# Conv taps, mean and activation at other places in the hand-written order of a two-layer hybrid trunk

## The chip, the cores and the metric

The kernel runs on one core of one Trainium2 chip. The metric is device time in microseconds (us) of one execution, compared by medians of several runs. The core has five engines with a queue of instructions each, which an engine works through in order: PE (matrix products; its weight loads are listed apart as PEld), DVE (vector operations), ACT (scalar functions, copies, squares), POOL and SP. SP's queue issues nearly all loads. [...]

## What is computed

Two layers. Each has a mixer with three branches that read the same normalised input h, each branch under a gate of its own, and then a gated feed-forward part with a width-3 convolution:

```
h = modulate(rms_norm(x, mix_norm_g[l]), sh1, sc1)
z = h @ w_in        # -> MLA latents, MoBA qkv, conv input, 3*D gate logits
o_a = causal_attention(...) @ w_mla_o                    # MLA branch
o_b = moba_attention(...) @ w_moba_o                     # MoBA branch
u = glu_a * sigmoid(glu_g)                               # conv branch
u = causal_depthwise_conv(u, conv_dw_w, conv_dw_b)       # width 31, 512 channels
u = silu(layer_norm(u, conv_ln_g, conv_ln_b))
o_c = u @ w_conv_pw2 + b_conv_pw2
merged = g[0] * o_a + g[1] * o_b + g[2] * o_c            # g = sigmoid(gate logits)
x = x + g1 * (merged @ w_out)
x = x + g2 * channel_mixer(modulate(rms_norm(x, ffn_norm_g[l]), sh2, sc2))
```

D is 1024, the sequence 256, the batch 1, all float32. `sh1, sc1, g1, sh2, sc2, g2` come from `silu(c) @ w_mod[l] + b_mod[l]`, one row of 6 × 1024 for each layer.

## The kernel before

Activations lie transposed on the chip, channels on the 128 partitions and the 256 positions along the row. Every float32 product is made of three: a weight tile and an activation are each split in a high part and a remainder, and PE forms high × high (L300), remainder of the activation × high weight (L301) and high × remainder of the weight (L303). Weights come in units of 512 KB (128 × 1024): SP loads one into one of four buffers `raw` (L199), ACT writes its high part `whi` (L222), DVE the remainder `wlo` (L224), three units ahead of the one in use. A unit of the gates is 24 matmuls on PE.

What stands where is written by hand: `STEPS` is one list of tokens for each layer, and the program is emitted in that order; the framework then orders each engine's queue by it and by what waits for what. Tokens that matter here:

- G51 is the first half of gate pair 5 (one unit), C31 a unit of the conv branch's gate, O5 a unit of the MLA and MoBA output products (`out_ab`), OC0 a pw2 product of the conv branch (`out_c`, four k-steps that read `uh` and `ul`), PR0 a step of the product with w_out. BA and MA are the two attentions, RW prepares the row `crow`.
- v0 and v1 mark a stretch of the list. `_spread` puts the conv's taps into it, 4 taps a token, evenly by the units of PE work. A tap is one DVE instruction (L1103); the 124 taps of a layer are 4 channel blocks × 31.
- r0 and r1 mark the stretch of the row products R: DVE multiplies a row of w_mod with `crow` and sums it (L390), then adds the bias (L391). There are 16 in layer 0 and 8 in layer 1 within the mixer. Each needs a load of 512 KB.
- m0 and m1 mark the stretch of M, four small matmuls of a k-step of the modulation (L407) on a tile `in_wm` that is loaded into a `raw` buffer.
- LN is `conv_mean`: three adds on DVE (L1113 to L1115), the mean by a matmul (L1116), four subtractions on DVE (L1121). LS is `conv_rstd`: four squares on ACT, three adds on DVE (L540, L535, L540), a sum over channels on PE (L545), L519 on DVE, a power on POOL (L520). LB is `conv_silu`: the broadcast on PE (L555), then for each of four blocks L1135 and L1140 on DVE around ACT's tanh, `uh` on ACT (L1141) and `ul` on DVE (L1142).

So the conv branch runs as a chain between DVE, PE and ACT while PE goes on with units of gates and outputs; where its instruction on PE comes up before DVE has delivered, PE stands.

Of the kernel before, what the change touches and what calls it, by code (L numbers as in the profile page):

```python
# [76 lines left out]
    "GLU0 GLU1 GLU2 GLU3 LE0 LE1 LR0 QKV00 LR1 LT QKV01 QKV02 QKV03 UQ UK QKV10 MS0 QKV11 MS1 QKV20 QKV12 "  # L77
    "QKV13 QKV21 MP0 MP1 m0 QKV22 v0 MA00 MA01 MA10 MA02 BS0 MA03 MA04 C00 MA11 BS1 BP0 BP1 QKV23 C01 MA12 "
    "MA13 C10 BA00 BA01 C11 MA14 BA02 G00 C20 BA03 BA10 BA11 BA12 C21 C30 BA13 G01 G10 G11 O0 G20 RW0 G21 G30 "
    "O1 O2 G31 G40 G41 O3 v1 RW1 RW2 RW3 O4 G50 C31 LN G51 G60 O5 LS G61 r0 LB O6 G70 G71 OC0 PR0 OC1 OC2 O7 "  # L80
    "OC3 OC4 PR1 PR2 OC5 m1 PR3 PR4 OC6 OC7 PR5 PR6 PR7 r1 "
), (
    "GLU0 GLU1 GLU2 GLU3 KL0 KL1 KL2 KL3 KL4 KL5 KL6 KL7 LE0 LE1 LR0 QKV00 LR1 LT QKV01 UQ QKV02 UK QKV03 MS0 "
    "QKV10 QKV11 v0 QKV12 MS1 QKV13 QKV20 MP0 QKV21 QKV22 MP1 QKV23 BS0 m0 MA00 MA10 C00 MA01 BS1 MA02 C01 MA11 "
    "MA03 C10 MA04 MA12 m1 C11 MA13 BP0 C20 BP1 MA14 C21 BA00 BA01 G00 BA02 BA10 G01 BA03 BA11 G10 v1 "
    "BA12 C30 G11 C31 BA13 O0 O1 G20 RW0 LN G21 G30 RW1 RW2 RW3 G31 O2 G40 r0 G41 G50 O3 LS G51 LB G60 O4 O5 G61 "
    "OC0 G70 OC1 PR0 OC2 OC3 PR1 OC4 OC5 G71 O6 O7 PR2 OC6 PR3 OC7 PR4 r1 PR5 PR6 PR7 "
)]

# [1335 lines left out]
```

## Time and profile before

| | us |
|---|---|
| median of 3 runs | 907.75 |
| lowest and highest | 905.73, 909.30 |
| the profiled execution, whole | 909.82 |
| its span between first and last instruction | 907.7 |

The profile's granted clock of PE has a mean of 0.996. The costliest groups of instructions are the weight split on ACT and DVE and the three product lines on PE:

```profile
L222 ACT ACTIVATE whi<-raw 128x1024 fp32r<-128x1024 f32 (+2 forms) x286 | 296.6, 1043 | 217.6 <-PE psb L301 117.3
L224 DVE TENSOR_TENSOR wlo<-raw,whi 128x1024 fp32r<-128x1024 f32 (+2 forms) x286 | 340.3, 1195 | 65.5 <-ACT whi L222 57.9
L300 PE MATMUL psb<-hh,whi 128*128 128x256 f32 x1088 | 263.5, 282 | 0.5 <-ACT p L675 0.3
L1103 DVE SCALAR_TENSOR_TENSOR cacc<-upad,cw,cacc 128x256 f32<-128x256 f32 x240 | 105.7, 477 | 0.4
```

A row reads: line, engine, operation, result and operands, shape, how often; busy us and mean ns of one; idle time of the engine just before such an instruction, and what ended most of it. A matmul's busy time overlaps the next one's, so the distance from one start to the next says more of PE. In a timeline, a row gives start and duration in us, and in brackets the idle time ahead of it with what ended it.

### The profile page before, as it was taken

Reading aid. Unit: us, or ns where it says so; the run is one execution under the profiler, and the core shown is the slowest. Engines: PE = TensorE matmul, PEld = TensorE weight load, DVE = VectorE, ACT = ScalarE, POOL = GpSimd, SP = SyncE. Lnnn points to the kernel's source line nnn. Section 1 sums busy time; section 2 is a strip of 40 time slices with the busy share of each in tenths; the row PEclk is TensorE's granted clock in tenths of the full one; section 3 lists DMA queues with packets and bytes.
Section 4 is the critical chain, followed back from the end, with each engine's and each line's share of the span. In section 5 each row is a group of like instructions: output and inputs, shape, how many; then the busy total and the mean of one; then the engine's idle time right before and its main releaser. Section 6 shows DMA issues by size and latency. Waiting matters only on the chain.

```text
span 907.7 us, 18736 instructions
## 1 busy us (share of the span) xinstructions
PE 888.3 (98%) x7339; PEld 841.5 (93%) x7339; DVE 797.1 (88%) x1554; ACT 555.2 (61%) x979; POOL 46.2 (5%) x36
## 2 busy tenths in 40 slices
PE   7999999999999999999999999999999999999998
PEld 6888888999998999999989988989999899999998
DVE  6989999999988999998764999999887798777774
ACT  4677588644755655556543676986475565565551
POOL 1010700000000000000000043000000000000000
PEclk9999999999999999999999999999999999999999
DMA  8956535699988889996633664157768676566631
GB/s 321 379 196 202 187 118 183 214 334 320 304 292 308 295 296 312 313 301 211 200 112 108 197 223 161 53 184 244 264 206 270 221 259 189 186 194 199 190 92 47
DMA packets 57976, 201.59 MB, mean 222 GB/s; under 512 B 6944, under 2 KB 8480, under 8 KB 57888
## 3 DMA queue, kind: packets, MB, share of 16 engines
q1 hardware_dynamic: 57888, 200.41, 66.6%
q8 instruction: 57, 0.93, 0.4%
q14 instruction: 31, 0.25, 0.1%
HBM read 199.33 MB, written 1.05 MB: 221 GB/s over the span
## 4 chain that ended last, share of the span: by engine, by line
PE 78%; DVE 12%; ACT 4%; DMA 3%; issue 2%; SPq 0%; POOL 0%; POOLq 0%; DVEq 0%; ACTq 0%
PE psb L300 16%; PE psb L301 16%; PE psb L303 15%; PE psa L300 7%; PE psa L301 7%; PE psa L303 7%; DVE wlo L224 3%; DVE cacc L1103 3%; PE psa L407 2%; DVE raw L778 1%; ACT whi L222 1%; PE psa L294 1%; DVE raw L390 1%; DMA raw<-in_win 1%; ACT p L675 1%
## 5 line engine op out<-in xcount | busy, mean ns | idle before, releaser
L222 ACT ACTIVATE whi<-raw 128x1024 fp32r<-128x1024 f32 (+2 forms) x286 | 296.6, 1043 | 217.6 <-PE psb L301 117.3
L224 DVE TENSOR_TENSOR wlo<-raw,whi 128x1024 fp32r<-128x1024 f32 (+2 forms) x286 | 340.3, 1195 | 65.5 <-ACT whi L222 57.9
L300 PE MATMUL psb<-hh,whi 128*128 128x256 f32 x1088 | 263.5, 282 | 0.5 <-ACT p L675 0.3
L301 PE MATMUL psb<-hl,whi 128*128 128x256 f32 x1088 | 261.0, 280 | 0.0
L300 PEld LDWEIGHTS psb<-hh,whi 128*128 128x128 f32 x1088 | 205.0, 189 | 6.3 <-issue 3.8
L301 PEld LDWEIGHTS psb<-hl,whi 128*128 128x128 f32 x1088 | 205.0, 189 | 0.5 <-DVE wlo L224 0.4
L303 PE MATMUL psb<-hh,wlo 128*128 128x256 f32 x1088 | 149.2, 279 | 0.0
L303 PEld LDWEIGHTS psb<-hh,wlo 128*128 128x128 f32 x1088 | 135.6, 188 | 0.8 <-issue 0.8
L1103 DVE SCALAR_TENSOR_TENSOR cacc<-upad,cw,cacc 128x256 f32<-128x256 f32 x240 | 105.7, 477 | 0.4
L300 PE MATMUL psa<-mhl,whi 128*128 128x256 f32 x400 | 94.0, 278 | 0.0
L301 PE MATMUL psa<-mhl,whi 128*128 128x256 f32 x400 | 93.7, 278 | 0.0
L1300 DVE SCALAR_TENSOR_TENSOR e<-psb,fw,e 128x255 f32<-128x255 f32 (+1 forms) x176 | 84.0, 477 | 5.4 <-ACT e L1298 4.5
L520 POOL TENSOR_TENSOR rs<-rs,mhalf 128x8 f32<-128x8 f32 (+3 forms) x26 | 44.6, 1729 | 669.2 <-DVE rs L519 669.1
L300 PEld LDWEIGHTS psa<-mhl,whi 128*128 128x128 f32 x400 | 75.0, 188 | 0.0
L301 PEld LDWEIGHTS psa<-mhl,whi 128*128 128x128 f32 x400 | 75.0, 188 | 0.0
L1298 ACT ACTIVATE e<-psb,fb,fw 128x256 f32<-128x256 f32 x88 | 48.5, 551 | 22.4 <-DVE e L1300 19.2
L390 DVE SCALAR_TENSOR_TENSOR raw<-raw,crow 128x1024 f32<-128x1024 f32 x48 | 58.5, 1218 | 0.5 <-DMA raw<-in_wmr 0.5
L303 PE MATMUL psa<-mhl,wlo 128*128 128x256 f32 x400 | 53.9, 277 | 0.0
L303 PEld LDWEIGHTS psa<-mhl,wlo 128*128 128x128 f32 x400 | 49.4, 188 | 0.0
L1308 ACT ACTIVATE mhl<-e 128x256 fp32r<-128x256 f32 x44 | 18.3, 416 | 30.1 <-DVE e L1306 27.6
L300 PE MATMUL psb<-whi,hh 128*128 128x416 f32 (+1 forms) x96 | 30.9, 350 | 4.5 <-ACT hh L854 4.5
L301 PE MATMUL psb<-whi,hl 128*128 128x416 f32 (+1 forms) x96 | 29.6, 343 | 0.2 <-DVE hl L855 0.2
(275 smaller groups left out, 1474.3 us busy)
## 6 DMA issues: line engine op xcount, KB each, us to landing
raw<-in_wup SPq DMA_DIRECT2D x88, 512.0 KB, 4.9
raw<-in_wmr SPq DMA_DIRECT2D x60, 512.0 KB, 5.7
raw<-in_wdn SPq DMA_DIRECT2D x44, 512.0 KB, 4.5
raw<-in_wm SPq DMA_DIRECT2D x32, 512.0 KB, 4.7
raw<-in_wgab SPq DMA_DIRECT2D x32, 512.0 KB, 4.9
raw<-in_wqkv SPq DMA_DIRECT2D x24, 512.0 KB, 5.1
raw<-in_win SPq DMA_DIRECT2D x16, 512.0 KB, 4.7
raw<-in_wgc SPq DMA_DIRECT2D x16, 512.0 KB, 4.3
```

The source lines that it names most:

```text
L222: ac.activation(hi, raw, AF.Copy)
L224: ve.tensor_tensor(lo, raw, hi.bitcast(F32), op=ALU.subtract)
L300: te.matmul(o, p1[0], p1[1], start=start, stop=False)
L301: te.matmul(o, p2[0], p2[1], start=False, stop=False)
L303: te.matmul(o, p3[0], p3[1], start=False, stop=stop)
L390: ve.scalar_tensor_tensor(raw, raw, scale, row, op0=ALU.mult, op1=ALU.mult, accum_out=acc)
L407: te.matmul(acc[32 * c:32 * c + 32, 0:S], cact[:, k:k + 1].to_broadcast([P, 32]), raw[:, c * S:(c + 1) * S], start=(k == 0), stop=(k == KD ...
L520: gp.tensor_tensor(r, r, mhalf[:, :n], op=ALU.pow)
L1103: ve.scalar_tensor_tensor(aj, upad[:, j, t:t + S], cw[:, j * 31 + t:j * 31 + t + 1], aj, op0=ALU.mult, op1=ALU.add)
L1298: ac.activation(t, src, AF.Identity, scale=fw[:, 2, c:c + 1], bias=fb[:, c:c + 1])
L1300: ve.scalar_tensor_tensor(t[:, d:S], src[:, 0:S - d], fw[:, 2 - d, c:c + 1], t[:, d:S], op0=ALU.mult, op1=ALU.add)
L1308: ac.activation(mh, th, AF.Copy)
```

## The change

Only the two lists change; no instruction is added or taken away.

```diff
@@ layer 0 @@
-    "O1 O2 G31 G40 G41 O3 v1 RW1 RW2 RW3 O4 G50 C31 LN G51 G60 O5 LS G61 r0 LB O6 G70 G71 OC0 PR0 OC1 OC2 O7 "
+    "O1 O2 G31 G40 G41 O3 v1 RW1 RW2 RW3 O4 G50 C31 G51 LN G60 O5 G61 LS r0 O6 LB G70 G71 OC0 PR0 OC1 OC2 O7 "
@@ layer 1 @@
-    "MA03 C10 MA04 MA12 m1 C11 MA13 BP0 C20 BP1 MA14 C21 BA00 BA01 G00 BA02 BA10 G01 BA03 BA11 G10 v1 "
-    "BA12 C30 G11 C31 BA13 O0 O1 G20 RW0 LN G21 G30 RW1 RW2 RW3 G31 O2 G40 r0 G41 G50 O3 LS G51 LB G60 O4 O5 G61 "
+    "MA03 C10 MA04 MA12 m1 C11 MA13 BP0 C20 BP1 MA14 C21 BA00 BA01 G00 BA02 BA10 G01 BA03 BA11 G10 "
+    "BA12 C30 G11 C31 BA13 O0 O1 G20 RW0 G21 G30 RW1 RW2 RW3 v1 G31 O2 LN G40 r0 G41 G50 O3 LS G51 LB G60 O4 O5 G61 "
```

In layer 0 the conv's mean (LN) goes behind G51, its variance (LS) behind G61, its activation (LB) behind O6. In layer 1 the taps are spread up to RW3 in place of G10, and LN goes from behind RW0 to behind O2.

PE in layer 0, the rows around the sum of squares L545 as they stand now. `raw_2944` is the tile of the modulation's next k-step, `oah` an operand of O6:

```order
L301 MATMUL psb_2717<-hl_136,whi_2676 128x256
L303 MATMUL psb_2717<-hh_135,wlo_2677 128x256 x8
L407 MATMUL psa_1377<-raw_2944,cact 32x256 x4
L545 MATMUL psb_2813<-ones,e_486_2814 128x1 x2
L300 MATMUL psb_2836<-oah_815,whi_2720 128x256
```

and the place where the same L407 stood before, between the two halves of gate pair 7:

```order
L303 MATMUL psb_2913<-hh_135,wlo_2751 128x256 x8
L407 MATMUL psa_1377<-raw_2944,cact 32x256 x4
L300 MATMUL psb_2913<-hh_135,whi_2800 128x256
L301 MATMUL psb_2913<-hl_136,whi_2800 128x256
L300 MATMUL psb_2913<-hh_135,whi_2800 128x256
```

The L407 has moved from behind O6 and G70 to ahead of L545 and O6.

DVE in layer 0, the stretch from the first L1135 of the activation to the first L1142, before (`ul` is what pw2 reads, `wlo` the weight remainders, `m` the row sums):

```order
L1135 TENSOR_TENSOR e_494_2835<-cacc_1297,psb_2830 128x256
L224 TENSOR_TENSOR wlo_2874<-raw_2871,whi_2873 128x1024
L1135 TENSOR_TENSOR e_497_2844<-cacc_1297,psb_2830 128x256
L1140 SCALAR_TENSOR_TENSOR e_496_2839<-e_495_2837,e_496_2839 128x256
L391 TENSOR_TENSOR mod_100<-m_599_3371,modb 128x1
L390 SCALAR_TENSOR_TENSOR raw_3328,m_607_3402<-raw_3328,crow_2273 128x1024
L1142 TENSOR_TENSOR ul_2834<-e_496_2839,uh_2833 128x256
```

and the rows that now lead to the first L1142:

```order
L390 SCALAR_TENSOR_TENSOR raw_3328,m_607_3402<-raw_3328,crow_2273 128x1024
L519 TENSOR_SCALAR rs_2827<-psb_2813 128x2
L391 TENSOR_TENSOR mod_100<-m_607_3402,modb 128x1
L390 SCALAR_TENSOR_TENSOR raw_3369,m_612_3451<-raw_3369,crow_2273 128x1024
L390 SCALAR_TENSOR_TENSOR raw_3400,m_619_3466<-raw_3400,crow_2273 128x1024
L1163 SCALAR_TENSOR_TENSOR b_484_2811<-b_484_2811,psb_2836 128x512
L1135 TENSOR_TENSOR e_502_2877<-cacc_1297,psb_2872 128x256
L1166 TENSOR_TENSOR mq_2604<-b_484_2811 128x256
L224 TENSOR_TENSOR wlo_2917<-raw_2914,whi_2916 128x1024
L1140 SCALAR_TENSOR_TENSOR e_504_2881<-e_503_2879,e_504_2881 128x256
L1135 TENSOR_TENSOR e_505_2886<-cacc_1297,psb_2872 128x256
L224 TENSOR_TENSOR wlo_2958<-raw_2955,whi_2957 128x1024
```

The row product of `raw_3328` stood right ahead of the first L1142; now it stands ahead of L519, and two later ones (`raw_3369`, `raw_3400`) are ahead of the activation as well. From the L1163 on `b_447` (ahead of the mean) to the fourth L1142 there stood 6 L390, 6 L391 and 9 L224; now 9, 10 and 10.

DVE in layer 1, the end of the mean's adds before:

```order
L224 TENSOR_TENSOR wlo_8190<-raw_8187,whi_8189 128x1024
L1166 TENSOR_TENSOR mq_8151<-b_1379_8071 128x256
L1114 TENSOR_TENSOR e_1400_8221<-cacc_7028 128x256
L224 TENSOR_TENSOR wlo_8233<-raw_8230,whi_8232 128x1024
L1115 TENSOR_TENSOR e_1399_8220<-e_1399_8220,e_1400_8221 128x256
```

and now:

```order
L1103 SCALAR_TENSOR_TENSOR cacc_7028<-upad_6551,cw_4342,cacc_7028 128x256 x3
L1114 TENSOR_TENSOR e_1417_8352<-cacc_7028 128x256
L1163 SCALAR_TENSOR_TENSOR b_1352_7869<-b_1352_7869,psb_8106 128x512
L224 TENSOR_TENSOR wlo_8141<-raw_8138,whi_8140 128x1024
L1166 TENSOR_TENSOR mq_8132<-b_1352_7869 128x256
L1163 SCALAR_TENSOR_TENSOR b_1379_8044<-b_1379_8044,psb_8144 128x512
L224 TENSOR_TENSOR wlo_8179<-raw_8176,whi_8178 128x1024
L1166 TENSOR_TENSOR mq_8132<-b_1379_8044 128x256
L1115 TENSOR_TENSOR e_1416_8351<-e_1416_8351,e_1417_8352 128x256
L390 SCALAR_TENSOR_TENSOR raw_8457,m_1449_8548<-raw_8457,crow_8210 128x1024
```

Of the weight splits one fewer stands ahead of L1115 (before, `wlo_8233` was between L1114 and L1115), and the row product of `raw_8457`, which stood ahead of the last taps, now stands behind it. On PE, L1116 moved from behind G21 to behind O2, three units later.

## Prediction before the run

> **What bounds the kernel now.** I read the busy shares first, then the chain that ended last, then windows of 10 us, then the timeline at each PE gap.
>
> ```profile
> PE 888.3 (98%) x7339; PEld 841.5 (93%) x7339; DVE 797.1 (88%) x1554; ACT 555.2 (61%) x979; POOL 46.2 (5%) x36
> PE 78%; DVE 12%; ACT 4%; DMA 3%; issue 2%; SPq 0%; POOL 0%; POOLq 0%; DVEq 0%; ACTq 0%
> ```
>
> PE carries 78% of the chain, so a change of order pays only where PE stands still. DVE's 88% is an average; the stages that the change touches are these:
>
> ```profile
> 200.00:210.00 10.00, 10.00 (x91) 10.00 (x90) 9.92 (x17) 4.10 (x5) 0.00 (x0) 1.00 0.94 336
> 210.00:220.00 10.00, 9.25 (x81) 8.62 (x80) 9.04 (x20) 5.42 (x9) 0.00 (x0) 1.00 0.91 308
> 220.00:230.00 10.00, 9.93 (x84) 9.76 (x84) 10.00 (x23) 6.53 (x10) 0.87 (x1) 1.00 0.97 346
> 630.00:640.00 10.00, 9.01 (x76) 8.79 (x75) 9.73 (x19) 5.54 (x9) 0.00 (x0) 1.00 0.79 254
> ```
>
> The columns after the length are PE, PEld, DVE, ACT and POOL busy, the granted clock, the DMA share and GB/s. The second and fourth rows hold the two conv means: PE is short by 0.75 and 0.99 us there, while DVE is full and the granted clock is 1.00. Around the conv's end two engines are at their limit at once, PE and DVE. The gaps themselves:
>
> ```profile
> 210.39 0.64 PE L407 MATMUL psa<-raw,cact 128*32 128x256 f32 x8
> 211.78 0.67 PE L1116 MATMUL psb<-e,mean_w 128*128 128x256 f32 x2 [0.75 <-DVE e L1115]
> 220.30 0.63 PE L303 MATMUL psb<-obh,wlo 128*128 128x256 f32 x4
> 221.00 0.58 PE L545 MATMUL psb<-ones,e 128*128 128x1 f32 x4
> 631.13 0.61 PE L303 MATMUL psb<-hh,wlo 128*128 128x256 f32 x4
> 632.73 0.67 PE L1116 MATMUL psb<-e,mean_w 128*128 128x256 f32 x2 [0.99 <-DVE mod L391]
> 587.27 0.28 PE L301 MATMUL psb<-hl,whi 128*128 128x256 f32 x1
> 587.92 0.63 PE L1013 MATMUL psa<-ident,mq 128*128 128x128 f32 x4 [0.38 <-DVE mq L623]
> ```
>
> A busy record overlaps the next one, so I take a loss from start to start. With 84 to 91 matmuls in 10 us (rows above) four run 0.46 us: L303 at 631.13 could have been followed at 631.59 and was followed at 632.73, a loss of **1.15 us**. L407 at 210.39 was followed 1.39 later; where nothing was waited for, a group of L407 was followed after 0.57 (230.63 and 231.20, quoted below), so this one lost **0.8 us**. L545 at 221.00 came 0.70 after four matmuls, a loss of **0.25 us**. L1013 came 0.65 after one matmul that takes 0.11, a loss of about **0.55 us**.
>
> **Layer 0, what goes.** The mean's wait (0.8) and the L545 wait (0.25) go with the old order, and I add 0.15 for small waits on `ul`: 1.2 us.
>
> **Layer 0, what comes.** The tokens alone look harmless, but row products (L390) are spread from r0 on, one share behind each unit, and O6 now stands between r0 and LB; so the program order of DVE has more of them ahead of the conv's end. Between the same L1163 (`b_447`, the first row below) and the last `ul` (L1142) stand now 9 L390, 10 L224 and 10 L391, before 6, 9 and 6, and four tiny ones (L509, L611).
>
> ```profile
> 206.47 0.67 DVE L1163 SCALAR_TENSOR_TENSOR b<-b,psb 128x512 f32<-128x512 f32 x1
> 210.08 1.21 DVE L390 SCALAR_TENSOR_TENSOR raw<-raw,crow 128x1024 f32<-128x1024 f32 x1
> 211.22 0.41 DVE L1115 TENSOR_TENSOR e<-e,e 128x256 f32<-128x256 f32 x1
> 219.30 1.22 DVE L224 TENSOR_TENSOR wlo<-raw,whi 128x1024 fp32r<-128x1024 f32 x1
> 220.44 0.41 DVE L540 TENSOR_TENSOR e<-e,e 128x256 f32<-128x256 f32 x1
> 220.78 0.15 DVE L391 TENSOR_TENSOR mod<-m,modb 128x1 f32<-128x1 f32 x1
> 220.84 1.22 DVE L390 SCALAR_TENSOR_TENSOR raw<-raw,crow 128x1024 f32<-128x1024 f32 x1
> 234.74 0.42 DVE L1142 TENSOR_TENSOR ul<-e,uh 128x256 fp32r<-128x256 f32 x1
> ```
>
> From start to start, L390 takes 1.14 (210.08 to 211.22), L224 1.14 (219.30 to 220.44) and L391 0.07 (220.78 to 220.84). Three more L390 and one more L224 are 4.56 us, four L391 0.28, the tiny ones about 0.5 by the 0.15 of L391: **5.4 us** in all. DVE has no idle time to swallow it but the wait of nearly 1 us at the mean (busy 9.04 of 10). The last `ul`, ready at 234.74 + 0.42 = 235.16, comes at 239.6 if that wait goes whole and at 240.6 if it stays. I take 240.5, since L224 there waits for ACT's `whi` and not for the mean.
>
> Two things on PE meet this. First, L407 of the modulation's next weight tile now stands ahead of L545, two units of 24 matmuls earlier than before. Its tile is loaded into the buffer that an L224 frees:
>
> ```profile
> 220.55 0.33 SPq L199 DMA_DIRECT2D raw<-in_wm  x1
> DMA to landing us min/median/max: 5.5/5.5/5.5
> 230.63 0.64 PE L407 MATMUL psa<-raw,cact 128*32 128x256 f32 x8
> 231.20 0.39 PE L300 MATMUL psb<-hh,whi 128*128 128x256 f32 x1
> ```
>
> The load left SP at 220.55, right after the L224 at 219.30 had ended (220.52), and took 5.5 us. That L224 comes, by the counts ahead of it, 0.5 us sooner to 0.6 us later, so the tile lands between 225.5 and 226.6. PE gets there after the L407 at 210.39 (0.57), four units of 24 matmuls and the mean (0.32, its two passes from 211.78 to 212.10). A unit is 24 × 10/91 to 24 × 10/84 = 2.64 to 2.86 us. So PE is there at 221.8 to 222.7 and stands **2.8 to 4.8 us**; I take 3.5. Before, this load had 230.63 − 226.05 = 4.6 us in hand. L545 behind it costs nothing more: its sum on DVE (L540, 5.4 us of work behind that L224) is ready near 226.5.
>
> Second, the pw2 product needs all four `ul`:
>
> ```profile
> 235.33 0.40 PE L301 MATMUL psb<-ul,whi 128*128 128x256 f32 x2
> 238.39 0.28 PE L300 MATMUL psb<-oah,whi 128*128 128x256 f32 x1
> ```
>
> Before, its last `ul` was used at 235.33, 0.17 us after it was made, and the next unit (O7) began at 238.39. With 1.2 us of stalls gone and 3.5 added, PE would begin O7 at 240.7; but behind the last `ul` at 240.5 there are still 15 matmuls of the three pw2 products, 15 × 0.117 = 1.75 us and a start, so 242.4. **Layer 0: 242.4 − 238.4 = +4.0 us**, of which 1.7 are new waits on `ul`. Since DVE's sum sets 242.4, the size of the L407 wait matters little. Bounds: −1.2 if both new waits are hidden (L407 late on PE by another cause, rows no longer ahead), +5.5 if DVE also waits for the transfer of one row (1.5 us, worked out with the rivals). On the other queues nothing is won or lost: POOL's one power (L520) moves with LS and its queue is empty (0.87 us busy in 220 to 230), and SP keeps the order of the unit loads, since no unit token changes its place.
>
> **Layer 1.** Taps from v0 to v1 are spread over nine more units, and L1116 moves on PE from behind G21 to behind O2 (three units, 3 × 2.75 = 8.3 us). PE comes to it at about 631.6 + 8.3 = 639.9. On DVE all 120 taps still lie ahead of L1114, but one L224 and one L390 fewer ahead of L1115:
>
> ```profile
> 632.16 0.42 DVE L1115 TENSOR_TENSOR e<-e,e 128x256 f32<-128x256 f32 x1
> 641.99 0.42 DVE L540 TENSOR_TENSOR e<-e,e 128x256 f32<-128x256 f32 x1
> 653.03 0.50 PE L545 MATMUL psb<-ones,e 128*128 128x1 f32 x4
> 667.95 0.28 PE L301 MATMUL psb<-ul,whi 128*128 128x256 f32 x1
> ```
>
> So L1115 ends near 632.6 − 2.3 = 630.3, over 9 us ahead of PE: **−1.15 us**. Of the MoBA rope (L1002, L622, L623) 22 to 23 taps now stand later, 22 × 0.40 = 8.8 us of DVE, so L623 is early and the 0.55 at 587.92 goes: **−0.55 us**. What becomes late next: on DVE seven L390 and four L224 now stand between L1115 and the four L1121 (630.3 + 11 × 1.14 + about 0.9 of small ones = 643.7), which end near 645; three L224 and three adds (3 × 1.14 + 3 × 0.34 = 4.4) lead from there to the last L540, so 649.5, and 650.5 with the waits for the squares on ACT. PE reaches L545 at 653.03 − 1.15 − 0.55 − 0.4 = 650.9. That slack was 653.03 − 642.41 = 10.6 us and is now 0.4 to 1.4, so I keep 0 to +1 for it and take 0. LS and LB and the pw2 product keep their places; `ul` is bound to them.
>
> There is one smaller term. After each mean stall PE ran slower at a granted clock of 1.00:
>
> ```profile
> 190.00:210.00 20.00, 20.00 (x179) 19.46 (x178) 19.91 (x36) 8.44 (x9) 0.00 (x0) 1.00 0.91 321
> 634.00:654.00 20.00, 20.00 (x172) 20.00 (x172) 18.39 (x36) 9.79 (x13) 0.00 (x0) 1.00 0.80 275
> ```
>
> 172 against 179 matmuls in 20 us: 4%, 0.8 us. If the stall starts it, half or all goes; I take −0.4. **Layer 1: −1.15 −0.55 −0.4 = −2.1 us**, bounds −3.0 (all of the slow stretch and other 0.4 us gaps of the attention) and −0.2 (a new wait at L545, slow stretch kept).
>
> **Sum.** +4.0 − 2.1 = +1.9 us. The profiled execution took 909.82 us (span 907.7, the other 2.1 outside of it), so it would show 911.7. The median shown, 907.75, is 2.07 below; the difference carries over: **909.6 us**, own range 907.9 to 911.4 (layer 0 at +3.1 to +4.1, layer 1 at −3.0 to −0.5).
>
> **Rivals.** *Both stalls go and nothing comes* (0.20): −1.2 − 2.1 = −3.3, 904.4; to 902.7 if layer 0's slow stretch (0.8) goes too and layer 1 gives 3.0. For it: the tokens alone say this. Against it: the rows on DVE, which the order shows. *The rows starve DVE* (0.20), the slower side: DVE is in order, so an L390 whose row has not landed holds every `ul` behind it. Three more rows in the same stretch are 3 × 524,288 bytes at 346 GB/s = 4.5 us of transfers. The DMA share is 0.91 to 0.97 there, so they have no room of their own. It decides once rows land later than DVE reaches them: +1.9 + 4.5 = +6.4, 914.2. Against it:
>
> ```profile
> L390 DVE SCALAR_TENSOR_TENSOR raw<-raw,crow 128x1024 f32<-128x1024 f32 x48 | 58.5, 1218 | 0.5 <-DMA raw<-in_wmr 0.5
> ```
>
> The 48 row products had 0.5 us of idle time before them in the whole span. *The order changes little* (0.08): DVE is full either way and PE stands at another place for as long, 908. *PE's stop drops its clock* (0.10): the profile has one such dip inside,
>
> ```profile
> 460.00:470.00 10.00, 9.67 (x87) 8.05 (x89) 6.63 (x16) 4.42 (x10) 0.70 (x1) 0.90 0.42 143
> 470.00:480.00 10.00, 10.00 (x106) 8.11 (x102) 6.90 (x16) 4.54 (x10) 0.00 (x0) 0.92 0.10 30
> ```
>
> worth (0.10 + 0.08) × 10 = 1.8 us; with the stop of 3.5 us at L407 the sum is +3.7, 911.5. The stops of about 1 us at the two means left the clock at 1.00. [...]
>
> **How the numbers follow.** Forecast 0.42, clock dip 0.10, little 0.08, gains only 0.20, starved rows 0.20. A measurement of this kernel can tell about 0.5%, 4.5 us, from no change. Faster: half of the gains case, 0.10. Slower: the starved rows and a little of the clock case at layer 0's upper bound, 0.23. Same: 0.67. The range 903.5 to 914.5 leaves out the ends of the gains and of the starved case, about 0.15.
>
> **What would show it.** Right: no wait at either L1116; a PE wait of about 3.5 us before the L407 ahead of L545, released by DMA; waits on `ul` (L1142) near 236 to 241; no wait at L1013. Wrong: L407 without a wait (its load came earlier), the last `ul` before 238, a DVE wait on `in_wmr` rows, a wait at the L545 of layer 1, or a granted clock below 1.00 near 226.

## The result and the profile after

| | before | changed |
|---|---|---|
| median of 4 runs, us | 908.05 | 915.87 |
| lowest to highest, us | 905.73 to 909.30 | 914.53 to 917.50 |
| profiled execution, us | 909.82 | 914.53 |
| span, us | 907.7 | 912.4 |

The changed kernel is slower: ratio 1.0083, 95% interval 1.0061 to 1.0105, or +7.8 us by the medians. The two profiled executions differ by 4.7 only: that of before lies 1.8 above its median and that of the changed kernel 1.3 below. The one of before has a dip of the granted clock between 460 and 480 (0.90 and 0.92, quoted in the prediction) that the changed kernel's lacks.

First the stretch of layer 0 in windows of 10 us (PE, PEld, DVE, ACT and POOL busy, granted clock, DMA share, GB/s):

```profile
210.00:220.00 10.00, 10.00 (x90) 9.41 (x89) 9.60 (x20) 5.13 (x9) 0.00 (x0) 1.00 0.89 303
220.00:230.00 10.00, 5.04 (x38) 4.03 (x38) 8.28 (x19) 2.77 (x4) 0.04 (x1) 0.75 0.86 305
230.00:240.00 10.00, 10.00 (x68) 10.00 (x68) 6.72 (x12) 4.50 (x7) 1.64 (x1) 0.74 0.68 240
240.00:250.00 10.00, 8.60 (x61) 7.31 (x60) 9.52 (x30) 7.00 (x14) 0.00 (x0) 1.00 0.54 176
```

The wait at the mean is gone (PE 10.00 in 210 to 220). Behind it PE does 38 matmuls in 10 us where it did 84, then 68 where it did 88, at a "full" 10.00: the granted clock is 0.75 and 0.74. DVE, full here before, is at 8.28 and 6.72. The timeline of PE shows where:

```profile
210.50 0.64 PE L407 MATMUL psa<-raw,cact 128*32 128x256 f32 x8
227.66 1.08 PE L407 MATMUL psa<-raw,cact 128*32 128x256 f32 x8 [4.96 <-DMA raw<-in_wm]
228.67 1.01 PE L545 MATMUL psb<-ones,e 128*128 128x1 f32 x4
234.81 0.77 PE L555 MATMUL psb<-ident,rs 128*128 128x128 f32 x4
242.59 0.38 PE L301 MATMUL psb<-ul,whi 128*128 128x256 f32 x1 [0.43 <-DVE ul L1142]
248.34 0.38 PE L300 MATMUL psb<-oah,whi 128*128 128x256 f32 x1 [0.34 <-ACT whi L222]
```

PE stands 4.96 us ahead of the L407, released by its tile's load, and O7 begins at 248.34 in place of 238.39. On the queues of SP and DVE:

```profile
221.38 0.33 SPq L199 DMA_DIRECT2D raw<-in_wm  x1
raw<-in_wm SPq DMA_DIRECT2D x1, 512.0 KB, 6.2
```

```profile
207.31 0.68 DVE L1163 SCALAR_TENSOR_TENSOR b<-b,psb 128x512 f32<-128x512 f32 x1
229.72 0.16 DVE L519 TENSOR_SCALAR rs<-psb 128x2 f32<-128x2 f32 x1 [1.73 <-PE psb L545]
235.12 0.69 DVE L1163 SCALAR_TENSOR_TENSOR b<-b,psb 128x512 f32<-128x512 f32 x1 [2.88 <-PE psb L303]
245.49 0.42 DVE L1142 TENSOR_TENSOR ul<-e,uh 128x256 fp32r<-128x256 f32 x1
```

The load left at 221.38 and took 6.2 us. DVE itself then waited for PE twice, 1.73 us for the sum of L545 and 2.88 us for O6, and the last `ul` was ready at 245.91. In windows of 1 us the clock reads:

```profile
224.00:225.00 1.00, 0.00 (x0) 0.00 (x0) 1.00 (x3) 0.00 (x0) 0.00 (x0) 0.95 0.92 295
225.00:226.00 1.00, 0.00 (x0) 0.00 (x0) 1.00 (x2) 0.00 (x0) 0.00 (x0) 0.50 1.00 393
...
234.00:235.00 1.00, 1.00 (x6) 1.00 (x6) 0.00 (x0) 0.45 (x1) 0.00 (x0) 0.50 1.03 422
235.00:236.00 1.00, 1.00 (x10) 1.00 (x9) 0.88 (x2) 0.00 (x0) 0.00 (x0) 0.93 0.60 246
```

Half clock from 224.9 to 235.1, about 10.2 us, of which PE stood still only for the first 2.7.

In layer 1 the waits that the change was to meet are gone:

```profile
589.83 0.49 PE L1013 MATMUL psa<-ident,mq 128*128 128x128 f32 x3
635.14 0.42 DVE L1115 TENSOR_TENSOR e<-e,e 128x256 f32<-128x256 f32 x1
646.27 0.60 PE L1116 MATMUL psb<-e,mean_w 128*128 128x256 f32 x2
655.18 0.43 DVE L540 TENSOR_TENSOR e<-e,e 128x256 f32<-128x256 f32 x1
657.61 0.50 PE L545 MATMUL psb<-ones,e 128*128 128x1 f32 x4
```

None of these rows of PE carries a bracket: L1115 is done 10.7 us ahead of L1116, and L540 is done at 655.61, 2.0 us ahead of L545. One wait has come in their place, at the transposes (L696) of an attention:

```profile
619.38 0.33 PE L696 MATMUL psa<-ident,p 128*128 128x128 f32 x1 [0.61 <-ACT p L687]
```

The stretch of layer 1 from its first attention product (L639) to its first pw2 product on `ul` took 105.4 us before, from 562.51 in the first row below to the 667.95 of the prediction. It takes 103.4 us in the changed kernel, from the second row to the third:

```profile
562.51 0.38 PE L639 MATMUL psa<-qkT 96*128 96x128 f32 x2
569.15 0.39 PE L639 MATMUL psa<-qkT 96*128 96x128 f32 x2
672.54 0.28 PE L301 MATMUL psb<-ul,whi 128*128 128x256 f32 x1
```

### The profile page after: what moved, and what is told of

Read it like the earlier page. It is cut to its first block, busy times and chain, and to the rows that moved or that the text cites. A ratio compares the mean times of both kernels' runs of the same rounds, so it can differ in the third digit from the quotient of the medians.

```text
span 912.4 us, 18740 instructions
## 1 busy us (share of the span) xinstructions
PE 888.3 (97%) x7339; PEld 841.3 (92%) x7339; DVE 797.2 (87%) x1554; ACT 553.7 (61%) x979; POOL 48.5 (5%) x36
## 4 chain that ended last, share of the span: by engine, by line
PE 79%; DVE 10%; DMA 4%; ACT 4%; issue 2%; SPq 0%; POOL 0%; POOLq 0%; DVEq 0%; ACTq 0%
PE psb L300 16%; PE psb L301 16%; PE psb L303 15%; PE psa L300 7%; PE psa L301 7%; PE psa L303 7%; DVE wlo L224 3%; DVE cacc L1103 2%; DMA raw<-in_wm 2%; ACT whi L222 2%; PE psa L407 2%; DVE raw L778 1%; PE psa L708 1%; PE psa L696 1%; ACT p L675 1%
## 5 line engine op out<-in xcount | busy, mean ns | idle before, releaser
L224 DVE TENSOR_TENSOR wlo<-raw,whi 128x1024 fp32r<-128x1024 f32 (+2 forms) x286 | 340.7, 1196 | 67.1 <-ACT whi L222 59.5
L520 POOL TENSOR_TENSOR rs<-rs,mhalf 128x8 f32<-128x8 f32 (+3 forms) x26 | 47.0, 1821 | 671.5 <-DVE rs L519 555.0
L1298 ACT ACTIVATE e<-psb,fb,fw 128x256 f32<-128x256 f32 x88 | 48.5, 551 | 30.5 <-DVE e L1300 27.5
L390 DVE SCALAR_TENSOR_TENSOR raw<-raw,crow 128x1024 f32<-128x1024 f32 x48 | 58.4, 1223 | 0.2 <-DMA raw<-in_wmr 0.2
```

The lines of the kernel that those rows point to most:

```text
L224: ve.tensor_tensor(lo, raw, hi.bitcast(F32), op=ALU.subtract)
L390: ve.scalar_tensor_tensor(raw, raw, scale, row, op0=ALU.mult, op1=ALU.mult, accum_out=acc)
L520: gp.tensor_tensor(r, r, mhalf[:, :n], op=ALU.pow)
L1298: ac.activation(t, src, AF.Identity, scale=fw[:, 2, c:c + 1], bias=fb[:, c:c + 1])
```

## Experiments

Times are medians, ratios stand against runs of the kernel before on the same chip in the same job. Two theories of the loss stood at the start: that PE's stop, with the clock behind it, is the loss, or that the row products on DVE are.

**Each layer's tokens alone** (`l0_only`, `l1_only`).

```diff
 l0_only: layer 0 as changed, layer 1 as before
 l1_only: layer 0 as before, layer 1 as changed
```

> Only the tokens of layer 0 are changed, layer 1 is that of before. Theory A (the loss lies in layer 0: PE stops 5 us at L407, its clock halves, the conv's chain comes late): the profile of the changed kernel is 9.7 us late at the end of this mixer and gets 1.5 back in the feed-forward part, so +8 to +11 us against before. Rival B (layer 0 costs about the +4 of the prediction and layer 1 costs the rest): +3 to +5 us.

> Only the tokens of layer 1 are changed. Theory A (layer 1 gains what its stalls cost): -2 to -4 us against before, no wait at the mean's matmul L1116 and none at L1013. Rival B (layer 1 costs): +2 to +4 us. Rival C: within 1 us.

Layer 0 alone: 916.66 us, ratio 1.0093 (1.0068 to 1.0119), +8.1. Layer 1 alone: 907.36 us, ratio 0.9984 (0.9963 to 1.0005), −1.2, not told apart from no change. The loss lies in layer 0.

**The tile's wait alone undone** (`m_behind`): L407 tied behind the last matmul of G70 (`lastmm`).

```diff
+        def mod_behind(g):
+            with tc.issue_after(lastmm[0].ins):
+                step(g)
```

> The changed kernel, with the one modulation step L407 whose tile came late tied behind the gate unit G70, where it stood before. Theory A (the load of this tile alone stops PE): the stop goes, the clock stays at 1.00, -7 to -9 us against the changed kernel. Rival B (DVE is just as late: the last L540 ended at 226.8, so PE would stand from 222.7 at L545): a stop of about 4 us at L545, a clock dip as before, only -1 to -3 us against the changed kernel.

916.13 us, ratio 1.0077 (1.0047 to 1.0107): nothing gained. PE stands at the next place, and the clock drops there too:

```profile
226.09 1.01 PE L545 MATMUL psb<-ones,e 128*128 128x1 f32 x4 [3.57 <-DVE e L540]
231.93 0.60 PE L555 MATMUL psb<-ident,rs 128*128 128x128 f32 x4
245.44 0.39 PE L300 MATMUL psb<-oah,whi 128*128 128x256 f32 x1 [0.27 <-ACT whi L222]
```

O7 began 2.9 us earlier than in the changed kernel. Later in this execution the clock was at half twice more, for 3.4 us each from 282.8 and from 293.0, and PE stood 1.70 us near 293 for another tile of the modulation. Theory A falls: L540 was late by itself, because DVE was.

**The clock alone** (`m_fill`, then `m_fill2`): 38 matmuls with zero weights (`fillat` is 38 there) behind G61, and L545 behind them, in the place of the stop; L407 is behind G70 as above.

```diff
+            if fillat[0]:
+                with tc.issue_after(lastmm[0].ins):
+                    for _ in range(fillat[0]):
+                        fl = te.matmul(macc[0][:, 0:S], maskb[:, 0:1].to_broadcast([P, P]), warm_w, start=False, stop=False)
```

> As m_behind, and 38 matmuls with zero weights (they add 0 to the open sum of the modulation) stand ahead of L545, about 4.1 us of PE work in the place of the stop. Theory A (half of the loss is the clock: half speed for about 10 us after the stop): granted clock 1.00 from 220 to 240, -4 to -6 us against m_behind. Rival B (the row products on DVE set the end of the conv whatever PE's clock): at most -1 us against m_behind.

916.73 us, ratio 1.0094 (1.0061 to 1.0127). The clock was 1.00 from 220 to 240 and 0.83 over 240 to 250 (3.4 us at half), but the fill had changed DVE's order: two more row products stood ahead of L519, which came at 230.49, 3 us behind the L545 that it waits for. So the run does not tell what the clock is worth. `m_fill2` ties DVE's order to that of `m_behind`:

```diff
+            with tc.issue_after(ul1[0].ins if used[0] > 14 else rst[0].ins) if l == 0 and used[0] > 12 else ExitStack():
                 use_row(fetched[used[0]], crow1[0], l, r, k, 0.5 if CDMA else 1.0)
```

> As m_fill, with the row products 14 to 16 and the next layer's tables tied so that DVE's order up to the last ul is that of m_behind, but for two sums of 0.07 us. Theory A (the half clock after the stop costs in itself): in m_behind the stretch from L545 to L555 took 5.8 us where full speed gives 3.4, and DVE then waited 1.6 us for PE; here the clock stays at 1.00, the last ul comes 1.5 to 2.5 us earlier than the 243.0 of m_behind, and O7 starts 1.5 to 2.5 us earlier than its 245.4. Rival B (the row products set the end by themselves): the last ul and O7 within 0.7 us of m_behind. Either way the stop itself is filled with work that is thrown away, so the time stays over that of before by at least 3 us.

914.26 us, ratio 1.0054 (1.0033 to 1.0075). From L545 (L550 here) to L555 (L560):

```profile
211.04 0.64 PE L407 MATMUL psa<-raw,cact 128*32 128x256 f32 x8
227.24 0.51 PE L550 MATMUL psb<-ones,e 128*128 128x1 f32 x4
230.57 0.60 PE L560 MATMUL psb<-ident,rs 128*128 128x128 f32 x4
244.30 0.38 PE L300 MATMUL psb<-oah,whi 128*128 128x256 f32 x1 [0.38 <-ACT whi L222]
```

3.3 us in place of 5.8. Counted from the L407 near 211, O7 begins 33.3 us later against 35.1 in `m_behind`: the half clock is worth 1.9 us at this place, as theory A had it, and the rest of the loss stays. This rests on two single executions: three traces with the same order in layer 0 (`before`, `l1_only`, `l1_ln`) have 28.0, 28.3 and 28.9 us for this distance. By the trace's own time O7 comes 1.1 us earlier (244.30 against 245.44), less than the 1.5 to 2.5 expected, and the intervals of the two ratios overlap.

**The rows ahead of `ul` without a stop** (`lb_only`).

```diff
-C31 LN G51 G60 O5 LS G61 r0 LB O6 G70
+C31 LN G51 G60 O5 LS G61 r0 O6 LB G70
```

> Layer 0 with LB alone moved behind O6 (LN and LS where they were), layer 1 as before. The scheduler leaves L407 behind G70, but 9 row products and 10 L224 stand ahead of the last ul, as in the changed kernel. Theory A (two causes in layer 0: rows ahead of ul, and the stop at L407 with its half clock): the first alone, so no stop, clock 1.00, the last ul 4.7 us later than before at 239 to 240, +3 to +5 us against before. Rival B (the rows cost nothing without the stop): within 1 us of before. Rival C (the rows are the whole loss): +7 to +9 us.

912.78 us, ratio 1.0041 (1.0011 to 1.0072), +4.9 by the medians.

```profile
211.72 0.64 PE L407 MATMUL psa<-raw,cact 128*32 128x256 f32 x8
222.72 0.58 PE L545 MATMUL psb<-ones,e 128*128 128x1 f32 x4
241.71 0.39 PE L301 MATMUL psb<-ul,whi 128*128 128x256 f32 x1 [0.48 <-DVE ul L1142]
244.08 0.39 PE L300 MATMUL psb<-oah,whi 128*128 128x256 f32 x1 [0.38 <-ACT whi L222]
```

No stop at L545, clock 1.00 to 280, and O7 begins 32.4 us after the L407, 4.4 us more than before (238.39 − 210.39 = 28.0). This is the term that the prediction worked out by counting on DVE. Up to 0.6 of the 4.4 is not rows: the wait at L1116, where the order is that of before, was 1.36 us in this execution and 0.75 in that of before. Theory A holds: the rows alone, without a stop, are about half of the 8.1 us of `l0_only`. That the other half is the stop and its clock follows by subtraction, and holds the new places of LN and LS too; no run shows it by itself.

**The row products held back** (`rows_ls`, `rows_lb`; `b_rows_ls`, `b_rows_lb` with layer 0 in the order of before and layer 1 as changed; `lastdve` is the last L540 or the last L1142).

```diff
+            with tc.issue_after(lastdve[0].ins) if l == 0 else ExitStack():
                 use_row(fetched[used[0]], crow1[0], l, r, k, 0.5 if CDMA else 1.0)
```

> The changed kernel, with the row products (L390, L391) of layer 0 tied behind the last L540 of LS. The scheduler then puts L407 behind G70 again by itself. Theory A (the row products pulled ahead on DVE are the root of both the late tile and the late L540): the last L540 ends near 221, no wait at L545, clock 1.00 from 220 to 240, the last ul near 236 to 238, -7 to -9 us against the changed kernel, 907 to 909. Rival B (moving LN, LS and LB behind a further unit costs by itself): at most -3 us.

> The changed kernel, with the row products of layer 0 tied behind the last ul (L1142) and r0 behind LB. Theory A: no wait on ul either, the last ul near 230 to 233, -8 to -10 us against the changed kernel, less what 16 row products (19 us of DVE) then cost late in the layer, where DVE has 6 to 7 us free before 283: a new wait of up to 3 us there. Rival B: at most -3 us.

> Layer 0 in the order of before, its row products tied behind the last L540; layer 1 as changed. Theory A: the wait at L1116 (0.75) shrinks since one row product fewer stands ahead of L1115, and the wait at L545 goes: 0 to -2 us against the run with layer 1 alone, 905 to 907. Rival B (these waits never cost anything): no difference.

> Layer 0 in the order of before, its row products tied behind the last ul, r0 behind LB; layer 1 as changed. Theory A: as the last one, and the last ul near 230: -1 to -3 us against the run with layer 1 alone, less a new wait of up to 3 us late in the layer. Rival B: the row products are late at the layer's end and it is slower, +1 to +4 us.

913.88 us (1.0043, 1.0023 to 1.0063), 921.76 (1.0128, 1.0089 to 1.0167), 913.93 (1.0044, 1.0022 to 1.0067) and 920.95 (1.0123, 1.0086 to 1.0160). All four are slower than before. Of the 7 to 10 us that the first two were to gain on the changed kernel, about 3 came with the first (+5.0 us over before, where the changed kernel has +7.8); the second is 5 us slower than the changed kernel (+12.9). The other two were to come out within 4 us of layer 1 alone at worst and are about 6 and 13 us over it. The windows of `rows_ls` say why:

```profile
210.00:220.00 10.00, 10.00 (x89) 9.40 (x89) 5.64 (x10) 5.40 (x9) 0.00 (x0) 1.00 0.72 239
220.00:230.00 10.00, 10.00 (x87) 9.86 (x86) 9.90 (x20) 4.91 (x7) 1.61 (x1) 1.00 0.73 240
...
250.00:260.00 10.00, 9.96 (x85) 9.76 (x84) 9.95 (x19) 5.39 (x10) 0.00 (x0) 1.00 0.93 326
260.00:270.00 10.00, 10.00 (x91) 9.78 (x91) 10.00 (x20) 5.40 (x7) 0.00 (x0) 1.00 0.95 363
270.00:280.00 10.00, 8.55 (x72) 6.84 (x64) 9.07 (x23) 4.41 (x11) 0.00 (x0) 1.00 0.90 315
280.00:290.00 10.00, 9.26 (x83) 6.45 (x83) 6.92 (x22) 5.75 (x12) 0.70 (x1) 0.83 0.69 238
```

At the conv the theory is right in the main: no stop at L407 or L545, clock 1.00 to 280, L540 done at 220.91; but the last `ul` was ready at 239.98, where 236 to 238 was expected. DVE idled 4.4 us in 210 to 220, where its rows had been, and is full from 240 to 270 (before it was at 8.1 and 7.8 in 250 to 270); PE then waits at the sum of the norm behind the mixer:

```profile
PE psb L545 <- DVE e L540: 1.7, 2, 1.5
```

(us in all, times, longest). With the rows behind the last `ul` (`rows_lb`) these waits are 4.4 us at L294 for `mhl` and 2.7 us at L545. In `b_rows_ls` PE waits 2.7 us near 191 for L1163 and 3.5 us near 279 for L540. So the rows ahead of the conv's end were filling DVE's free time ahead of it; DVE has none left between 240 and 270, and what is put off comes back as a wait behind it.

**LN alone** (`ln_l1`: layer 0 with LN behind G51 only; `l1_ln`: layer 1 with LN behind O2 but the taps spread up to G10).

```diff
 ln_l1, in layer 0
-C31 LN G51 G60 O5 LS G61 r0 LB O6 G70
+C31 G51 LN G60 O5 LS G61 r0 LB O6 G70
 l1_ln, against the kernel before
-G10 v1 BA12 C30 G11 C31 BA13 O0 O1 G20 RW0 LN G21 G30 RW1 RW2 RW3 G31 O2 G40
+G10 v1 BA12 C30 G11 C31 BA13 O0 O1 G20 RW0 G21 G30 RW1 RW2 RW3 G31 O2 LN G40
```

> Layer 0 with LN alone moved behind G51, layer 1 as changed. One row product more than before stands ahead of the last ul (7), and one of the four matmuls of the L407 now stands ahead of L555. Theory A: the wait at L1116 in layer 0 goes (0.8 us) and the last ul is 1.2 us later, a wait of 2 to 3 us at the L407 matmul or at L545 comes: 0 to +3 us against the run with layer 1 alone. Rival B (only the wait at the mean counted): -1 us.

> Layer 0 as before; in layer 1 LN behind O2 but the taps spread up to G10 as before. Theory A (LN takes away the wait at the mean, the taps' spread that at the rope): no wait at L1116, the wait of 0.4 us at L1013 is still there. Rival B (the spread does both): the wait at L1116 stays.

`ln_l1`: 912.98 us, ratio 1.0054 (1.0031 to 1.0077), +5.1 us over before and about 6 over layer 1 alone, where 0 to 3 was expected.

```profile
214.75 0.60 PE L1116 MATMUL psb<-e,mean_w 128*128 128x256 f32 x2
226.41 0.61 PE L545 MATMUL psb<-ones,e 128*128 128x1 f32 x4 [2.85 <-DVE e L540]
228.95 1.06 PE L407 MATMUL psa<-raw,cact 128*32 128x256 f32 x2 [1.72 <-DMA raw<-in_wm]
```

The wait at the mean is gone and two waits of 4.6 us in all have come for it, with the clock at half for 6.8 us. So LN alone costs about 6 us and LB alone about 5, and LN, LS and LB together 8.1: the costs do not add. `l1_ln`: 907.07 us, ratio 0.9989 (0.9969 to 1.0008). L1116 shows no wait, L1013 one of 0.24:

```profile
588.16 0.63 PE L1013 MATMUL psa<-ident,mq 128*128 128x128 f32 x4 [0.24 <-DVE mq L623]
```

So moving LN takes away the one and the spread of the taps the other, as theory A said. But the spread gains nothing by it: a wait of 0.45 to 0.63 us at L696 is in all ten traces that have it, and in the other four none above 0.17. From the first L639 of layer 1 to its first pw2 product on `ul` three traces with layer 1 as before have 104.6 to 105.4 us, the ten with both changes 103.4 to 104.1, and `l1_ln` with LN alone has 103.4. How the spread makes L696 late is not shown.

No version was shown to be faster than the kernel before in the medians; the two with layer 1's change or part of it alone (`l1_only`, `l1_ln`) have the right sign, within their intervals.

## Why the prediction was wrong

It forecast +1.9 us and 903.5 to 914.5; measured were +7.8 and 915.87. By its steps:

- **The program order decides, and rows are pulled ahead: right.** The DVE sum of 5.4 us held: from `b_447` to the last `ul`, less its waits, DVE took 27.7 us before and 33.2 now. The run with LB alone, which has these rows and no stop, put O7 4.4 us later where the prediction had +4.0.
- **The stop at L407: right in kind, short in size.** 4.96 us against 3.5 (bounds 2.8 to 4.8): the load took 6.2 us, not 5.5, and left SP at 221.38, 0.2 us behind the latest time that the prediction allowed.
- **"Since DVE's sum sets 242.4, the size of the L407 wait matters little": this step failed.** It took DVE's sum as running free of PE. L519 needs PE's L545 and L1163 needs PE's O6, so the stop came back on DVE: 1.73 + 2.88 = 4.6 us of waits. The same sum with them fits: last `ul` at 240.5 as predicted, + 0.8 since `b_447` began at 207.31 and not 206.47, + 4.6 = 245.9, measured 245.91. With it the new order of layer 0 costs twice what the sum had.
- **The clock: named as a rival at 0.10 and 1.8 us; it happened and lasted longer.** The price was read off a dip of one stretch of 3.4 us. After a stop the half clock lasted 10.2 us here, and 6.8 us each in `l0_only`, `m_behind` and `ln_l1`. The two cannot simply be added, since a slower O6 (229.55 to 234.81, 5.3 us, where it took 3.0 before) is part of DVE's wait; `m_fill2` against `m_behind` gives 1.9 us at O7 for one of 6.8 us.
- **"L545 behind it costs nothing more": right in the changed kernel.** Its last L540 was done at 226.78, where the prediction had 226.5, and the L407 came at 227.66. What the prediction did not draw from this is that L545 is nearly as late as the tile: with L407 out of the way it stops PE for 3.57 us. Both waits have one root, DVE being late with what stands ahead of them.
- **Layer 1: −2.1 predicted, −1.2 measured** (−3.4 to +0.5 by the interval). Each wait that was to go is gone; the new wait at L545 that was kept as 0 to +1 did not come (2.0 us of slack). The −0.55 for the rope was not gained, since the spread brought the wait at L696, which the prediction did not have. The medians do not settle the size; the traces, with 104.6 to 105.4 against 103.4 to 104.1 us in the stretch above, say 0.5 to 2.0 us.
- **Layer 0 in the sum:** +4.0 predicted, with bounds of −1.2 and +5.5; +8.1 measured with it alone (+6.2 to +10.8 by the interval).

From the L407 near 210 to the start of O7, read from each timeline:

| kernel | us | against before |
|---|---|---|
| rows held behind the last `ul` (`rows_lb`) | 27.5 | −0.5 |
| before | 28.0 | |
| rows held behind L540 (`rows_ls`) | 30.7 | +2.7 |
| rows ahead of `ul`, no stop (`lb_only`) | 32.4 | +4.4 |
| the stop at L545 filled (`m_fill2`) | 33.3 | +5.3 |
| LN alone moved, stops of 2.9 and 1.7 us (`ln_l1`) | 34.3 | +6.3 |
| stop of 3.6 us at L545, half clock (`m_behind`) | 35.1 | +7.1 |
| layer 0 as changed (`l0_only`), stop of 4.3 us | 36.4 | +8.4 |
| changed, stop of 5.0 us | 37.8 | +9.8 |

The distance to O7 is not the whole loss: `rows_lb` is early there and 12.9 us slower at the end.

The rival with starved rows came nearest in time (914.2), by luck: it had the right sign and the wrong mechanism. The row products waited for their rows 0.8 us or less in all in every trace but that of `m_fill`, which has three waits of 2.3 us together.

## What to carry to other kernels

Where two engines are both full and hand a chain to and fro, a sum of one engine's instructions is a lower bound only (4.6 us of waits for PE came on top of DVE's sum here); walk the chain through both, and let a stop on one come back as a wait on the other. Moving a wait on the busiest engine is worth its length only if what stands behind it is early by as much, and putting work off a full engine pays only if that engine has free time later, before the result is needed. Price a stop of several us on PE at its length and the half clock that came with it here: 6.8 us of it with the stops of 3.6 and 4.3 us, 10.2 with that of 5.0, but 3.4 with that of 4.4 us in `rows_lb`.

## What the hardware showed unasked

- The granted clock fell to 0.50 in or within 1 us behind the stops of 4.96 (changed kernel), 4.4 (`rows_lb`), 4.29 (`l0_only`), 3.57 (`m_behind`) and 3.5 us (`b_rows_ls`). For shorter stops the length alone does not tell: the clock stayed at 1.00 through stops of 2.28 (changed kernel, ahead of 25.25), 1.78 (before, ahead of 18.39) and 1.36 us (`lb_only`), and fell at stops of 2.85 (`ln_l1`), 2.7 (`rows_lb`), 1.70 (`m_behind`) and 0.33 us (before, ahead of 468.04).
- The half clock lasted 3.4 us in some stretches (before from 468.09, `lb_only` from 280.74, `l0_only` from 284.84, `m_behind` from 282.76 and 293.00, `rows_lb` from 274.00), 6.8 in others (`l0_only` from 226.81, `m_behind` from 224.73, `ln_l1` from 227.30, `rows_lb` from 284.24) and 10.2 in the changed kernel (from 224.90). Where a trace has several, their starts lie whole multiples of 3.41 us apart: in `m_behind` 17 and 3 times, in `l0_only` 17 times, in `rows_lb` 3 times. In the 6.8 us of `l0_only`, `m_behind` and `ln_l1` and the 10.2 us of the changed kernel PE was busy again for most of the time: in the changed kernel from 228.0 on without a gap, and the clock came back at 235.14; in `m_behind` from 226.1 on, and it came back at 231.56. Why is open.
- At the norm between mixer and feed-forward part of layer 0, between 280 and 289, the clock fell to half for 3.4 us in the profiled executions of `l0_only`, `m_behind`, `lb_only`, `rows_ls` and `m_fill2` (a mean of 0.83 over 280 to 290 in each), and not in those of the changed kernel and of `ln_l1` (1.00 from 270 to 300), nor in that of the kernel before (1.00 from 20 to 460). Layer 0 has the same order in the changed kernel and in `l0_only`. So a single profile holds or lacks about 1.7 us (3.4 us at half clock) there with no change of order, and two profiles can differ from two medians by that much. What decides it is not shown.
